# Attention products of the meta tokens and the indexer on 128 contraction rows, and a narrower pooling input

## The chip, the cores and the metric

The kernel runs on one core of a Trainium2 chip. The metric is the device time of one execution in microseconds; a lower time is better. Engines are named as in the profile: PE (TensorE, matmuls), PEld (its weight loads), DVE (VectorE), ACT (ScalarE), POOL (GpSimd), SP (SyncE, which issues the large DMAs).

## What is computed

One layer of a decoder on 256 tokens behind 16 learned meta tokens (272 in all, L), width 2048, in float32. The part that matters here:

```
h = rms_norm(x); q, c_kv, q_idx, k_idx, w_idx, p_in, g_a, g_b = split(h @ w_in)
# indexer: 8 heads of 64; each query keeps the 68 best keys
score[t,s] = sum_h w_idx[t,h] * relu(q_idx[t,h] . k_idx[s] * 64**-0.5), causal
# attention: 16 heads of 128, keys and values from the latent c_kv (256) by w_uk, w_uv
p = softmax(q . (c_kv @ w_uk) * 128**-0.5 over the kept keys);  o = p @ (c_kv @ w_uv)
# pooling: 4 groups of 256 channels, trailing means over 2, 4, 8, 16 tokens minus the token
y[t] = mean(p_in[t-w+1 .. t]) - p_in[t];  b = (y @ w_pool) * scale
merged = sigmoid(g_a) * (o @ w_attn_o) + sigmoid(g_b) * (b @ w_pool_o)
x = x + merged @ w_out;  x = x + relu(rms_norm(x) @ W1)**2 @ W2;  out = rms_norm(x)[16:]
```

## The kernel before

Float32 products are made of three matmuls of a shorter type: each operand is split into a high part (a rounded copy, made by ACT) and a low part (the rest, a subtraction on DVE or POOL), and the product is high x high + high x low + low x high, added up in PSUM. `mm3` (L143 to L146) issues these three; `split_psum`, `split_sbuf` and `split_pair` (L108 to L135) make the two parts of a result.

All weights come in units of 1 MB by SP into three raw buffers. A unit is cut into blocks; `split_block` (L215 to L244) makes a block's two parts, three blocks ahead of its matmuls (four buffers each for high and low). In blocks 20 to 111, POOL makes half of the low part. The last loop of the program walks the list of blocks in order: it converts block i + 3, takes small pieces of side work from a queue (`pop_side`, one piece per block), and issues block i's matmuls. So a piece of side work (normalization, index scores, top-k rounds, attention) stands in PE's queue between two blocks of a large projection, a "slab". Every engine works through its own queue in order.

`slab_t` (L279 to L313) multiplies a slab of 512 columns of weights, transposed, by the 16 chunks of h: per chunk and column tile a 512-wide and a 256-wide matmul (L302, L303), or, where the flag `wide` is set, three matmuls over all 272 tokens (L144 to L146 by `mm3`). Wide are the latent, the index keys and the 8 tiles of the pooling input.

The indexer: its queries (4 tiles, two heads of 64 rows each, `qi`) and its keys (64 rows, held twice in 128 partitions, `kw["k"]`) are split like all else. `score(h)` (L505 to L519) takes the 64 rows of one head, and for each of two query tiles (144 and 272 keys) issues `mm3`; heads are pieces of side work, one per block.

Attention: `kv_block(m)` (L583 to L618), one for each two heads, makes the keys, and the values in three pieces: 16 meta rows, 128 rows, 128 rows. It takes five PSUM banks in turn out of three, so that it waits for evictions. `push_attention` (L620 to L712) queues for each head the scores (s1), the exponentials (s1b), the scaling (s2), the transposition and split of the probabilities (s3, L657 to L676), and the product with the values (s4, L678 to L698): three matmuls on the 16 meta rows, three on the first 128 keys, three on the last 128 keys for the second half of the queries. s3 of one head and s2 of the next are one piece; s4 comes a step after s3.

Pooling: `done_p` (L769 to L776) scales a tile of the pooling input by the token's norm, over all 272 tokens; `pool_tile` (L778 to L802) sums neighbours in doubling steps on POOL.

Of the kernel before, what the change touches and what calls it, by code (L numbers as in the profile page):

```python
# [16 lines left out]
P = 128  # L17
D = 2048
KC = D // P
S = 256  # L20
# [57 lines left out]
def decoder_layer(ctx, tc, x, meta, g_mix, w_in, kv_g, ik_g, w_uk, w_uv, w_ao, w_pool,  # L78
# [11 lines left out]
    early = ExitStack()  # L90
    ptp = early.enter_context(tc.tile_pool(name="ptp", bufs=2))
    fpl = early.enter_context(tc.tile_pool(name="fpl", bufs=1))
    ecst = early.enter_context(tc.tile_pool(name="ecst", bufs=1))
# [185 lines left out]
    def slab_t(w, c0, tiles, rhs, nk=KC, done=None, wide=None, lead=False, more=None):  # L279
# [4 lines left out]
        def mm(k):  # L284
            def go(hi, lo):
                if k == 0:
                    st["ps"] = [gbank() for _ in range(tiles)]
                wides = [wide is not None and wide[j] for j in range(tiles)]
                pss = [st["ps"][j][:, 0:L] if wides[j] else st["ps"][j].rearrange("p (a n) -> p a n", a=2)
                       for j in range(tiles)]  # L290
                todo = [(j, kk) for j in range(tiles) for kk in range(2)]
                if k == 0 and lead:
                    todo.sort(key=lambda jk: jk[1])
                for j, kk in todo:
                    ps = pss[j]
                    xt, o = rhs(k + kk)
                    wh, wl = hi[:, kk, j * P:(j + 1) * P], lo[:, kk, j * P:(j + 1) * P]
                    f, l = k + kk == 0, k + kk == nk - 1
                    if wides[j]:
                        mm3(ps, wh, wl, xt[:, 0, :], xt[:, 1, :], f, l)  # L300
                    else:
                        T.matmul(ps, wh, xt[:, :, o:o + S], start=f, stop=False)  # L302
                        T.matmul(ps[:, 0], wl, xt[:, 0, o:o + S], start=False, stop=l)  # L303
                if k + 2 == nk:
                    jobs = [done(j, pss[j]) for j in range(tiles)]
                    wave(jobs + (more() if more else []))
            return go
# [79 lines left out]
    wn = [cst.tile([P, IH], F32, name=f"wn{t}") for t in range(2)]  # L387

    def done_a1(j, ps):
        if j == 0:  # L390
# [5 lines left out]
        if j == 3:  # L396
            push_kv_norm()
        return split_pair(t, ps)

# [45 lines left out]
    def done_a2(j, ps):  # L445
        if j < 2:
            t = slots.get()
            qi.append(t)
            return split_pair(t, ps)
        kw["raw"] = plain.get()  # L450
# [6 lines left out]
    def push_index():  # L457
# [36 lines left out]
        def s4():  # L494
            kf = env["sq"][:, 1, :]
            kw["k"] = slots.get()
            split_sbuf(kw["k"], kf, L)
            plain.put(env["sq"])
# [6 lines left out]
        def score(h):  # L505
            def go():
                rl = flat(env["rl"][h % 2])
                b = (h % 2) * IDIM
                q, k = qi[h // 2], kw["k"]
                ps = mbank()  # L510
                for t, c0, n in ((0, 0, N0), (1, N0, N1)):
                    qh = q[b:b + IDIM, 0, t * P:(t + 1) * P]
                    ql = q[b:b + IDIM, 1, t * P:(t + 1) * P]
                    mm3(ps[:, c0:c0 + n], qh, ql, k[b:b + IDIM, 0, 0:n], k[b:b + IDIM, 1, 0:n], True, True)
                for t, c0, n in ((0, 0, N0), (1, N0, N1)):
# [5 lines left out]
        def acc(h):  # L521
# [10 lines left out]
                if h == IH - 1:  # L532
# [5 lines left out]
                    for s in qi:  # L538
                        slots.put(s)
                    slots.put(kw["k"])  # L540
                    for s in env["rl"]:
                        plain.put(s)
# [33 lines left out]


    qT = {}
    oT = {}
# [3 lines left out]
    def kv_block(m):  # L583
# [5 lines left out]
        def go(hi, lo):  # L589
# [9 lines left out]
            for o, rows in ((0, NM), (NM, P), (NM + P, P)):  # L599
# [7 lines left out]
                t = slots.get()  # L607
                split_psum(t, ps[0:rows, :], S, rows)
                vv.append(t)
# [10 lines left out]
    def push_attention():  # L620
# [36 lines left out]
        def s3(h):  # L657
            def go():
                sm, _ = env[h]
                f = flat(sm)  # L660
                pt = ptp.tile([P, 2, 640], F32R, tag="pt", name="pt")
                ps = mbank()
# [6 lines left out]
                split_psum(pt, ps[:, 0:384], 384)  # L669
                ptf = pt.bitcast(F32)  # L670
                A.copy(pt[0:NM, 0, 384:640], pz[0:NM, 0:S])
                V.tensor_tensor(out=pt[0:NM, 1, 384:640], in0=pz[0:NM, 0:S], in1=ptf[0:NM, 0, 384:640],
                                op=ALU.subtract)
                plain.put(sm)
                env[h] = pt
            return go  # L676

        def s4(h):  # L678
            def go():
# [4 lines left out]
                o = slots.get()  # L684
                mm3(ps[:, 0:S], vm[0:NM, 0, e:e + DH], vm[0:NM, 1, e:e + DH],
                    pt[0:NM, 0, 384:640], pt[0:NM, 1, 384:640], True, False)
                mm3(ps[:, 0:S], v0[:, 0, e:e + DH], v0[:, 1, e:e + DH], pt[:, 0, 0:S], pt[:, 1, 0:S], False, False)
# [82 lines left out]
    def done_p(s):  # L770
        def go(j, ps):
            i = 4 * s + j
            if i % 2 == 0:
                praw.append(plain.get())
            return [scaled(praw[i // 2][:, i % 2, :], ps, L), lambda: pools.append(i)]
        return go  # L776

    def pool_tile(i):  # L778
# [3 lines left out]
        buf = [tmp[:, 0, :], tmp[:, 1, :]]  # L782
        cur, n, d = p, L, 1
        for lev in range(g + 1):
# [467 lines left out]


    slab_t(w_in, C_KV, 4, rhs_h, done=done_a1, wide=(1, 1, 0, 0), lead=True)
    slab_t(w_in, C_QI + 256, 3, rhs_h, done=done_a2, wide=(0, 0, 1))
    for s in range(3):
# [5 lines left out]
    for s in range(2):  # L1262
        slab_t(w_in, C_P + s * 512, 4, rhs_h, done=done_p(s), wide=(1, 1, 1, 1))
    for s in range(4):
# [158 lines left out]
```

## Time and profile before

| | |
|---|---|
| median of 3 runs | 1411.14 us (1410.97 to 1415.86) |
| the profiled execution | 1411.46 us, its span 1409.7 us |
| PE busy | 1391.6 us (99%), 7664 matmuls |
| PEld busy | 1195.6 us (85%) |
| DVE / ACT / POOL busy | 999.1 / 773.7 / 215.2 us |
| DMA | 264.64 MB, mean 188 GB/s |
| granted TensorE clock | 0.996 of full speed over the span |

The span is the time between the first and the last instruction of the profile. A matmul's busy time runs from its start to its end, and neighbouring matmuls overlap; the pace of a row of matmuls is the distance of their starts.

### The profile page before, as it was taken

What the parts mean: (1) busy time and instruction counts of PE and PEld (TensorE: products, weight loads), DVE (VectorE), ACT (ScalarE), POOL (GpSimd) and SP (SyncE); (2) the same over time, 40 slices, a digit from 0 to 9 for tenths busy, and PEclk for the clock granted to TensorE, in tenths of its full rate; (3) what the DMA queues carried; (4) which work ended last, traced back from release to release, by engine and by line L of the source; (5) the groups of instructions that cost most, each with busy time, mean ns of one, the idle gap of its engine ahead of it and who ended that gap; (6) DMA issues with size and microseconds to landing.
All of it is one profiled execution on the core that took longest, in us unless ns stands there. A gap on an engine that the chain in (4) does not pass through costs nothing.

```text
span 1409.7 us, 19906 instructions
## 1 busy us (share of the span) xinstructions
PE 1391.6 (99%) x7664; PEld 1195.6 (85%) x7664; DVE 999.1 (71%) x1511; ACT 773.7 (55%) x1208; POOL 215.2 (15%) x177
## 2 busy tenths in 40 slices
PE   9999999999999999999999999999999999999997
PEld 7888888899988888888888888888788887788886
DVE  5667965565568766665567887679767788977894
ACT  5655465555555744454465566455555556545562
POOL 1154454444406000000000010000110002000000
PEclk9999999999999999999999999999999999999999
DMA  6654544444446555564555578645787458665562
GB/s 228 198 176 150 165 150 156 145 134 150 150 150 222 200 183 179 198 213 179 179 180 166 196 235 242 204 167 194 220 238 229 157 202 247 236 206 168 195 221 100
DMA packets 125999, 264.64 MB, mean 188 GB/s; under 512 B 5222, under 2 KB 16528, under 8 KB 125904
## 3 DMA queue, kind: packets, MB, share of 16 engines
q1 hardware_dynamic: 120016, 251.68, 52.7%
q0 software_dynamic: 5856, 11.68, 4.1%
q8 instruction: 60, 0.98, 0.3%
q14 instruction: 35, 0.29, 0.1%
q10 hardware_dynamic: 32, 0.01, 0.0%
HBM read 252.86 MB, written 2.10 MB: 181 GB/s over the span
## 4 chain that ended last, share of the span: by engine, by line
PE 75%; issue 12%; DVE 8%; DMA 3%; ACT 1%; POOL 1%; DVEq 0%; ACTq 0%; POOLq 0%
PE g L302 29%; PE g L303 15%; PE g L332 3%; PE g L330 3%; PE g L331 3%; PE m L957 2%; PE m L959 2%; PE m L958 2%; DVE lo L241 2%; PE g L144 2%; PE g L146 2%; PE g L145 2%; PE m L144 1%; DMA raw<-in_w_mlp_out_dram 1%; DVE lo L239 1%
## 5 line engine op out<-in xcount | busy, mean ns | idle before, releaser
L302 PE MATMUL g<-r,hi 128*128 128x512 f32 x2240 | 791.8, 396 | 1.0 <-DVE f L131 1.0
L236 ACT CAST hi<-raw 128x1024 fp32r<-128x1024 f32 (+1 forms) x441 | 455.1, 1045 | 370.1 <-PE g L302 232.1
L303 PE MATMUL g<-r,lo 128*128 128x256 f32 x2240 | 630.5, 281 | 0.6 <-DVE lo L241 0.6
L241 DVE TENSOR_TENSOR lo<-raw,hi 128x1024 fp32r<-128x1024 f32 (+1 forms) x349 | 422.9, 1222 | 245.2 <-ACT hi L236 244.2
L302 PEld LDWEIGHTS g<-r,hi 128*128 128x128 f32 x2240 | 420.9, 188 | 98.2 <-DVE f L131 2.1
L303 PEld LDWEIGHTS g<-r,lo 128*128 128x128 f32 x2240 | 422.9, 189 | 1.1 <-DVE lo L241 0.9
L239 POOL TENSOR_TENSOR lo<-raw,hi 128x512 fp32r<-128x512 f32 x92 | 153.5, 1676 | 213.7 <-ACT hi L236 213.0
L239 DVE TENSOR_TENSOR lo<-raw,hi 128x512 fp32r<-128x512 f32 x92 | 85.4, 929 | 87.5 <-ACT hi L236 87.5
L1067 POOL DMA_DIRECT2D w<-w x32 | 27.8, 1080 | 550.0 <-ACT w L1064 427.5
L957 PE MATMUL m<-hi,r 128*128 128x512 f32 x224 | 89.5, 400 | 0.8 <-ACT w L1064 0.8
L959 PE MATMUL m<-hi,r 128*128 128x512 f32 x224 | 88.6, 396 | 0.0
L958 PE MATMUL m<-lo,r 128*128 128x512 f32 x224 | 88.4, 395 | 0.0
L958 PE MATMUL g<-lo,r 128*128 128x512 f32 x168 | 66.4, 395 | 2.5 <-DVE lo L241 2.3
L130 ACT COPY b<-g 128x256 f32<-128x256 f32 x148 | 54.7, 371 | 25.6 <-PE g L303 20.8
L957 PE MATMUL g<-hi,r 128*128 128x512 f32 x168 | 66.4, 395 | 0.0
L959 PE MATMUL g<-hi,r 128*128 128x512 f32 x168 | 66.4, 395 | 0.0
L330 PE MATMUL g<-hi,r 128*128 128x512 f32 x160 | 64.3, 402 | 0.0
L332 PE MATMUL g<-hi,r 128*128 128x512 f32 x160 | 63.3, 395 | 0.0
L331 PE MATMUL g<-lo,r 128*128 128x512 f32 x160 | 62.5, 390 | 0.0
L144 PE MATMUL g<-r,hi 128*128 128x272 f32 (+1 forms) x192 | 56.9, 296 | 0.0
L236 ACT CAST hi<-ta 128x1024 fp32r<-128x1024 f32 x28 | 29.4, 1051 | 47.8 <-DVE ta L986 29.2
L146 PE MATMUL g<-r,lo 128*128 128x272 f32 (+1 forms) x192 | 55.4, 289 | 0.0
(239 smaller groups left out, 1791.8 us busy)
## 6 DMA issues: line engine op xcount, KB each, us to landing
raw<-in_w_mlp_in_dram SPq DMA_DIRECT2D x64, 1024.0 KB, 5.5
raw<-in_w_mlp_out_dram SPq DMA_DIRECT2D x64, 1024.0 KB, 5.3
raw<-in_w_in_dram SPq DMA_DIRECT2D x56, 1024.0 KB, 5.1
raw<-in_w_attn_o_dram SPq DMA_DIRECT2D x16, 1024.0 KB, 5.1
raw<-in_w_out_dram SPq DMA_DIRECT2D x16, 1024.0 KB, 5.1
raw<-in_w_pool_o_dram SPq DMA_DIRECT2D x8, 1024.0 KB, 5.1
w<-w POOLq DMA_DIRECT2D x32, 256.0 KB, 8.2
raw<-in_w_in_dram SPq DMA_DIRECT2D x8, 512.0 KB, 8.4
```

What stands on the lines that cost most here:

```text
L144: T.matmul(ps, wh, xh, start=first, stop=False)
L236: A.copy(hv, src)
L239: e.tensor_tensor(out=lv[:, kk], in0=src[:, kk], in1=hv.bitcast(F32)[:, kk], op=ALU.subtract)
L241: V.tensor_tensor(out=lv, in0=src, in1=hv.bitcast(F32), op=ALU.subtract)
L302: T.matmul(ps, wh, xt[:, :, o:o + S], start=f, stop=False)
L303: T.matmul(ps[:, 0], wl, xt[:, 0, o:o + S], start=False, stop=l)
L330: T.matmul(ps, xh, hi[:, kk], start=f, stop=False)
L331: T.matmul(ps, xh, lo[:, kk], start=False, stop=False)
L332: T.matmul(ps, xl, hi[:, kk], start=False, stop=l)
L957: T.matmul(ps, xh, wh, start=first, stop=False)
L958: T.matmul(ps, xh, wl, start=False, stop=False)
L959: T.matmul(ps, xl, wh, start=False, stop=last)
```

## The change

The products of the meta tokens and of the index scores are laid out so that the parts of the split lie below each other in the partitions, and one matmul with 128 contraction rows adds up what were several.

- Index queries: `split_heads` puts a head's high and low part into the two halves of the 128 partitions of one plane (even heads plane 0, odd heads plane 1). The high part of the keys lies in both halves already; the low part goes to a second tile `z`, zero but for the half that meets the high queries. Two matmuls per query tile instead of three.
- Meta values: rows 0 to 31, 32 to 63 and 96 to 127 hold the high part (of which 16 rows count), rows 64 to 95 the low part. Meta probabilities go to one of two fixed tiles `pm`, zeroed once: high in rows 0 to 15 and 64 to 79, low in rows 32 to 47. One matmul instead of three.
- Pooling input: `wide` becomes a number of columns. A group with window w computes the last 256 + w tokens (258, 260, 264, 272), two tiles each; `done_p` and `pool_tile` follow.

```diff
@@ slab_t
-                wides = [wide is not None and wide[j] for j in range(tiles)]
-                pss = [st["ps"][j][:, 0:L] if wides[j] else st["ps"][j].rearrange("p (a n) -> p a n", a=2)
+                wides = [wide is not None and wide[j] > 0 for j in range(tiles)]
+                pss = [st["ps"][j][:, 0:wide[j]] if wides[j] else st["ps"][j].rearrange("p (a n) -> p a n", a=2)
...
-                        mm3(ps, wh, wl, xt[:, 0, :], xt[:, 1, :], f, l)
+                        mm3(ps, wh, wl, xt[:, 0, L - wide[j]:], xt[:, 1, L - wide[j]:], f, l)
@@ done_a1, done_a2: split_heads in place of split_pair
+    def split_heads(dst, ps):
+
+        t, st = pair(ps)
+        d = dst.bitcast(F32)
+        lo, hi = slice(0, IDIM), slice(IDIM, P)
+
+        def sub(o, a, b):
+            return lambda: V.tensor_tensor(out=dst[o, b, 0:S], in0=t[a], in1=d[a, b, 0:S], op=ALU.subtract)
+
+        return st + [lambda: A.copy(dst[lo, 0, 0:S], t[lo]), lambda: A.copy(dst[hi, 1, 0:S], t[hi]),
+                     sub(hi, lo, 0), sub(lo, hi, 1)]
@@ push_index, s4
-            split_sbuf(kw["k"], kf, L)
+            z = kw["z"] = slots.get()
+            V.memset(flat(z).bitcast(F32), 0.0)
+            A.copy(kw["k"][:, 0, :], kf)
+            for b, o in ((0, slice(0, IDIM)), (1, slice(IDIM, P))):
+                V.tensor_tensor(out=z[o, b, :], in0=kf[o], in1=kw["k"].bitcast(F32)[o, 0, :], op=ALU.subtract)
@@ score
-                b = (h % 2) * IDIM
-                q, k = qi[h // 2], kw["k"]
+                q, k, z = qi[h // 2], kw["k"], kw["z"]
                 ps = mbank()
                 for t, c0, n in ((0, 0, N0), (1, N0, N1)):
-                    qh = q[b:b + IDIM, 0, t * P:(t + 1) * P]
-                    ql = q[b:b + IDIM, 1, t * P:(t + 1) * P]
-                    mm3(ps[:, c0:c0 + n], qh, ql, k[b:b + IDIM, 0, 0:n], k[b:b + IDIM, 1, 0:n], True, True)
+                    o, qt = ps[:, c0:c0 + n], q[:, h % 2, t * P:(t + 1) * P]
+                    T.matmul(o, qt, k[:, 0, 0:n], start=True, stop=False)
+                    T.matmul(o, qt, z[:, h % 2, 0:n], start=False, stop=True)
@@ before kv_block
+    pms = [mtp.tile([P, S], F32R, name=f"pm{i}") for i in range(2)]
+    for t in pms:
+        V.memset(t.bitcast(F32), 0.0)
@@ kv_block
-                split_psum(t, ps[0:rows, :], S, rows)
+                if rows == NM:
+                    A.copy(t[0:32, 0, 0:S], ps[0:32])
+                    V.tensor_tensor(out=t[64:96, 0, 0:S], in0=ps[0:32], in1=t.bitcast(F32)[0:32, 0, 0:S],
+                                    op=ALU.subtract)
+                    for o in (32, 96):
+                        A.copy(t[o:o + 32, 0, 0:S], ps[0:32])
+                else:
+                    split_psum(t, ps[0:rows, :], S, rows)
@@ s3
-                pt = ptp.tile([P, 2, 640], F32R, tag="pt", name="pt")
+                pt = ptp.tile([P, 2, 384], F32R, tag="pt", name="pt")
...
-                A.copy(pt[0:NM, 0, 384:640], pz[0:NM, 0:S])
-                V.tensor_tensor(out=pt[0:NM, 1, 384:640], in0=pz[0:NM, 0:S], in1=ptf[0:NM, 0, 384:640],
+                pm_ = pms[h % 2]
+                A.copy(pm_[0:NM], pz[0:NM, 0:S])
+                V.tensor_tensor(out=pm_[32:32 + NM], in0=pz[0:NM, 0:S], in1=pm_.bitcast(F32)[0:NM],
                                 op=ALU.subtract)
+                A.copy(pm_[64:64 + NM], pz[0:NM, 0:S])
@@ s4
-                mm3(ps[:, 0:S], vm[0:NM, 0, e:e + DH], vm[0:NM, 1, e:e + DH],
-                    pt[0:NM, 0, 384:640], pt[0:NM, 1, 384:640], True, False)
+                T.matmul(ps[:, 0:S], vm[:, 0, e:e + DH], pms[h % 2], start=True, stop=False)
@@ done_p, pool_tile
-            return [scaled(praw[i // 2][:, i % 2, :], ps, L), lambda: pools.append(i)]
+            n = S + WIN[i // 2]
+            return [scaled(praw[i // 2][:, i % 2, L - n:], ps, n), lambda: pools.append(i)]
...
-        cur, n, d = p, L, 1
+        n, d = S + WIN[g], 1
+        cur = p[:, L - n:]
@@ the slabs
-        slab_t(w_in, C_P + s * 512, 4, rhs_h, done=done_p(s), wide=(1, 1, 1, 1))
+        slab_t(w_in, C_P + s * 512, 4, rhs_h, done=done_p(s), wide=[S + WIN[2 * s + j // 2] for j in range(4)])
```

## Rows read from the trace of the kernel before

**Rows 1.** First part of the page: busy us (share of the span) and instructions by engine.
```profile
PE 1391.6 (99%) x7664; PEld 1195.6 (85%) x7664; DVE 999.1 (71%) x1511; ACT 773.7 (55%) x1208; POOL 215.2 (15%) x177
```

**Rows 2.** Waits of PE: engine, line, releaser, total us, times, longest us.
```profile
PE m L604 <- DVE r L110: 1.7, 3, 1.1
```

**Rows 3.** Busy times by window: length, PE, PEld, DVE, ACT, POOL (instructions), clock, DMA.
```profile
160.00:200.00 40.00, 38.61 (x243) 34.38 (x242) 31.21 (x65) 21.57 (x42) 17.62 (x13) 1.00 0.57 192
```

**Rows 4.** Groups of PE by line and shape: weights, moving operand, count, busy us, mean ns.
```profile
L144 PE MATMUL m<-pt,r 16*128 16x256 f32 x16 | 6.1, 384 | 0.0
...
L144 PE MATMUL m<-r,r 64*128 64x144 f32 x8 | 2.6, 331 | 0.0
```

**Rows 5.** Timeline of PE, 256-column products near the end (start us, duration us); 18 steps.
```profile
1398.06 0.28 PE L352 MATMUL g<-r,r 128*128 128x256 f32 x1
...
1400.17 0.29 PE L352 MATMUL g<-hi,r 128*128 128x256 f32 x1
```

**Rows 6.** Timeline of PE, one head's value products between two slab matmuls.
```profile
232.27 0.28 PE L303 MATMUL g<-r,lo 128*128 128x256 f32 x1
232.47 0.39 PE L144 MATMUL m<-pt,r 16*128 16x256 f32 x1
...
233.49 0.22 PE L144 MATMUL m<-pt,r 128*128 128x128 f32 x1
...
233.77 0.45 PE L302 MATMUL g<-r,hi 128*128 128x512 f32 x1
```

**Rows 7.** Timeline of PE, index scores: the first head, then the last.
```profile
98.34 0.33 PE L145 MATMUL m<-r,r 64*128 64x144 f32 x1 [0.19 <-DVE r L114]
...
128.12 0.28 PE L303 MATMUL g<-r,lo 128*128 128x256 f32 x1
...
129.24 0.50 PE L302 MATMUL g<-r,hi 128*128 128x512 f32 x1
129.57 0.28 PE L303 MATMUL g<-r,lo 128*128 128x256 f32 x1
```

**Rows 8.** Timeline of PE, one head's attention scores up to the second slab matmul.
```profile
210.64 0.23 PE L144 MATMUL m<-r,r 128*128 128x144 f32 x1
...
210.83 0.27 PE L146 MATMUL m<-r,r 128*128 128x144 f32 x1
210.94 0.33 PE L144 MATMUL m<-r,r 128*128 128x272 f32 x1
...
211.35 0.40 PE L302 MATMUL g<-r,hi 128*128 128x512 f32 x1
211.59 0.28 PE L303 MATMUL g<-r,lo 128*128 128x256 f32 x1
```

**Rows 9.** Timeline of DVE: the fill at the start, the low part of the index keys.
```profile
0.84 0.17 DVE L152 MEMSET ones<- 128x128 f32 x1 [0.84 <-PEq L1410]
...
96.76 1.53 DVE L114 TENSOR_TENSOR r<-f,r 128x272 fp32r<-128x272 f32 x1
```

**Rows 10.** Timeline of PE, pooling input, 272 columns; 20 steps.
```profile
329.75 0.29 PE L144 MATMUL g<-r,hi 128*128 128x272 f32 x1
...
332.25 0.29 PE L146 MATMUL g<-r,lo 128*128 128x272 f32 x1
```

**Rows 11.** Groups of ACT by shape: busy us, mean ns, idle us before, releaser.
```profile
L654 ACT ACTIVATE f<-f,st 128x144 f32<-128x144 f32 x16 | 6.7, 416 | 19.2 <-DVE st L653 19.2
...
L671 ACT CAST pt<-m 16x256 fp32r<-16x256 f32 x16 | 5.7, 357 | 0.0
...
L109 ACT CAST r<-m 16x256 fp32r<-16x256 f32 x8 | 2.9, 362 | 1.9 <-PE m L606 1.9
```

**Rows 12.** Timeline of PE at the start, first transpose of the meta tokens.
```profile
6.82 0.23 PE L1344 MATMUL m<-ident,f 16*128 16x16 f32 x1 [0.62 <-DMA f<-in_meta_tokens_dram]
```

**Rows 13.** Timeline of PE and its weight loads at a slab matmul.
```profile
202.02 0.39 PE L302 MATMUL g<-r,hi 128*128 128x512 f32 x1
202.03 0.19 PEld L303 LDWEIGHTS g<-r,lo 128*128 128x128 f32 x1
```

More of the change, by code (lines that the diff above doesn't have):

```diff
@@ L91, in decoder_layer @@
     ptp = early.enter_context(tc.tile_pool(name="ptp", bufs=2))
+    mtp = early.enter_context(tc.tile_pool(name="mtp", bufs=1))
     fpl = early.enter_context(tc.tile_pool(name="fpl", bufs=1))
@@ L397, in done_a1 @@
             push_kv_norm()
-        return split_pair(t, ps)
+        return split_heads(t, ps)
     def push_kv_norm():
@@ L448, in done_a2 @@
             qi.append(t)
-            return split_pair(t, ps)
+            return split_heads(t, ps)
         kw["raw"] = plain.get()
@@ L540, in acc @@
                     slots.put(kw["k"])
+                    slots.put(kw["z"])
                     for s in env["rl"]:
@@ L669, in go @@
                 split_psum(pt, ps[:, 0:384], 384)
-                ptf = pt.bitcast(F32)
-                A.copy(pt[0:NM, 0, 384:640], pz[0:NM, 0:S])
-                V.tensor_tensor(out=pt[0:NM, 1, 384:640], in0=pz[0:NM, 0:S], in1=ptf[0:NM, 0, 384:640],
+                pm_ = pms[h % 2]
+                A.copy(pm_[0:NM], pz[0:NM, 0:S])
+                V.tensor_tensor(out=pm_[32:32 + NM], in0=pz[0:NM, 0:S], in1=pm_.bitcast(F32)[0:NM],
                                 op=ALU.subtract)
+                A.copy(pm_[64:64 + NM], pz[0:NM, 0:S])
                 plain.put(sm)
@@ L1251, in final @@
             nc.sync.dma_start(out=out[t * P:(t + 1) * P, s * 512:(s + 1) * 512], in_=f)
-    slab_t(w_in, C_KV, 4, rhs_h, done=done_a1, wide=(1, 1, 0, 0), lead=True)
-    slab_t(w_in, C_QI + 256, 3, rhs_h, done=done_a2, wide=(0, 0, 1))
+    slab_t(w_in, C_KV, 4, rhs_h, done=done_a1, wide=(L, L, 0, 0), lead=True)
+    slab_t(w_in, C_QI + 256, 3, rhs_h, done=done_a2, wide=(0, 0, L))
     for s in range(3):
```

## The prediction

> **What bounds the kernel now.** I read the busy times first: TensorE is busy for 1391.6 of 1409.7 us, and no other engine comes near it [rows 1]. A busy matmul is not yet a useful one, so the next view is the list of what TensorE waited for: the largest entry that touches the changed code is 1.7 us, in the value products of the key/value blocks, for VectorE [rows 2]. Then the stage in which most of the change lies, from 160 to 200 us: TensorE is busy for 38.61 of 40 us, ScalarE for 21.57, GpSimd for 17.62; only VectorE, with 31.21, is near [rows 3]. So the order of matmuls sets the time, and what an edit is worth is read from start to start of neighbouring matmuls in the timeline, not from their durations: these overlap, so that a removed product is worth far less than its duration, and a pause between two of them isn't in their durations at all. The reader is to see in that view that the matmuls on 16 and 64 rows stand apart from their neighbours by more than a product's pace.
>
> **Meta tokens, 16 heads.** Each head has three products on 16 contraction rows [rows 4] ahead of six on 128. The plain pace of a 256-column product on 128 rows is (1400.17 - 1398.06) / 18 = 0.117 us [rows 5]. From the slab matmul ahead of a head's products to the slab matmul behind them are 233.77 - 232.27 = 1.50 us [rows 6]; the other heads show the same within 0.02. After the change one product on 128 rows takes the place of the three. Then the same stretch is: five steps of 0.117 (slab matmul to meta product, to the three products of the first block of keys, to the first of the second block), and the 0.28 us that the last three products take now, from 233.49 to 233.77 [rows 6]; together 0.865. It saves 0.635 per head, 10.2 us in all. Of this only 2 x 0.117 are columns that are no longer streamed; 0.40 are pauses where the row count changes, at entering and at leaving the 16-row products. That they go is the step that carries the forecast.
>
> **Indexer scores, 8 heads.** Each head has six products on 64 rows [rows 4]; the change makes it four on 128. From the slab matmul ahead of them to the second slab matmul behind them are 129.57 - 128.12 = 1.45 us [rows 7]. For the time after, the trace has a pattern of the same widths on 128 rows, the attention scores: from their first product to the next slab matmul 211.35 - 210.64 = 0.71, then 0.24 to the second slab matmul [rows 8]. Two products go from it, one of 144 columns (0.11 from 210.83 to 210.94) and one of 272 (0.125, below), and 0.117 to enter come on: 0.117 + 0.71 - 0.11 - 0.125 + 0.24 = 0.83. It saves 0.62 per head. Seven heads give 4.3 us. The first head I count at nothing: today its second product waits for VectorE's subtraction (0.19 us idle at 98.34), which takes 1.53 us there, beside GpSimd [rows 7, 9]. After the change a zero fill of 544 columns and a second subtraction stand in the same VectorE queue. The fill is at most 544 / 128 x 0.17 = 0.7 us, an estimate from the fill of 128 columns [rows 9], the subtraction up to another 1.53, so this head may lose up to 1.6 or gain 0.6; nothing is in the middle. Behind it on VectorE stands a weight subtraction for a block some way ahead.
>
> **Pooling input.** Eight tiles take 16 x 3 products each of 272 columns; six of them get narrower, to 258, 260 and 264 columns, two tiles each, so 96 products of each width. At 272 columns the pace is (332.25 - 329.75) / 20 = 0.125 us, at 256 it was 0.117 [rows 5, 10], so 0.49 ns a column: 96 x (14 + 12 + 8) x 0.49 ns = 1.6 us. Below zero is open here: the moving operand then starts 14, 12 or 8 columns into its tile, which no product of this width does today; the last rival has that. The upper bound is these 1.6 us.
> By the Trainium skill (TensorE: Matmul & The Clock Gate, "Back-to-back issue gap") a warm product costs its columns at 2.4 GHz and 2.5 ns, 116 ns at 272 columns, where the trace has 125; the three widths would then be worth 96 x (5.8 + 5.0 + 3.3) ns = 1.4 us, an estimate, and the sum 0.2 us smaller. The trace decides.
>
> **What is added.** On ScalarE: a third copy of the meta probabilities per head, 16 x 0.357, two more copies of the meta values per key/value block, 16 x 0.362 [rows 11], and four more of half the rows where the indexer's queries are split, about 0.36 each: 13 us, spread from 30 to 410 us. The copy per head can be late at most until VectorE's subtraction before it is through; but ScalarE already stands there for VectorE, 19.2 us in 16 waits for the reciprocal that follows that subtraction [rows 11], so only its 0.36 us are new, ahead of weight casts that are made three blocks early. I cost it at nothing. The two copies in a key/value block stand ahead of the evictions of the two larger value banks, and all later weight casts. The next user of the meta bank is a block later. Their bounds are nothing and 8 x 0.72 = 5.8 us; I take 0.5, near the low end, since the three waits on these banks total only 1.7 us [rows 2] and ScalarE idles for 18 of 40 us there [rows 3]. VectorE's added subtractions for the queries (four of half the rows) lie in a stretch without a TensorE wait. The two zero fills of 256 columns at the start, at most 2 x 0.34 us by the same estimate, may push the warm-up matmuls back; they end well before the first meta transpose at 6.82, which waits 0.62 us for its DMA [rows 12]. No DMA is added, removed or moved.
>
> **Sum.** 10.2 + 4.3 + 0 + 1.6 - 0.5 = 15.6 us. The profiled execution took 1411.5 us (span 1409.7), 0.3 above the median of the three runs, so the forecast is 1395.9. What is late next is again TensorE; the chain of weight cast and subtraction has to run 4% faster between 160 and 410 us.
>
> **Rivals.** *The pauses stay* (they belong to freshly written operands, not to the row count): then only columns go, 32 x 0.117 + 7 x 0.235 + 1.6 - 0.5 = 6.5 us, 1405. Against it: the attention scores read fresh tiles too, and enter and leave at the plain pace [rows 8]. Chance 0.05.
> *ScalarE's copies reach TensorE*: the key/value blocks give back all of the 5.8 us, 1401. For it: VectorE, whose subtraction follows each cast, has 9 us of slack in 40 [rows 3], and a cast late by 0.7 us makes it later. Against it: ScalarE's slack. Chance 0.10.
> *The weight loads of the new products come bare*, each 0.19 us longer: 48 remaining new products (32 scores, 16 meta) x 0.19 = 9.1 us, gain 6.5, 1405. Today a load on 128 rows begins at 202.03, inside the product that began at 202.02 and lasts 0.39 [rows 13], so it is hidden. Chance 0.01. Such a rule stands in the Trainium skill (TensorE: Matmul & The Clock Gate, Part 3, "What overlaps and what doesn't"): a load overlaps with a running matmul only where their row groups differ. It speaks for small row groups and against this change; the trace does not agree with it.
> *The pooling products get slower*: if the odd start of the moving operand costs reading time, all 288 pay. Place: the two pooling slabs; the point from which it decides is (15.6 - 1.6) / 288 = 49 ns a product above today's 125. At a halved reading pace, 0.117 us more, it costs 33.7, and 14.0 - 33.7 gives 1431, slower. For it: nothing but that no row has such a start at this width; against it: the slab products already start 16 columns in and keep their pace. Chance 0.03.
> The forecast itself, gains of 12 to 19.5 us, holds 0.80; 0.01 is left for what I don't see.
>
> **Range and chances.** Low end: head 0 gains 0.6, no added cost, and the 1.7 us of waits shrink: 1411.5 - 16.1 - 0.6 - 1.7 = 1393, and 1392 with the reading error of the steps. High end: the second rival, 1401.5. Within 0.5% of the time before (7.1 us, about what a measurement of this kernel can tell from no change) means above 1404: the first and third rival. Faster 0.91 (forecast, second rival, the unseen), same 0.06, slower 0.03.
>
> **What will show it.** In the timeline after: slab matmul to slab matmul 0.87 around a head's value products, 0.83 around a head's index scores up to the second slab matmul, no larger step before the first 128-row product; pooling steps of 0.118 to 0.121. Matmuls fall by 16 + 32, to 7616. TensorE's waits on the value products show whether the 0.5 was right; a ScalarE cast as releaser of weight subtractions more often than now would speak for the second rival. The forecast is wrong if the steps around the changed products stay above 0.2 us, or if the pooling pace rises.

## The result and the profile after

The median of six runs after is 1399.24 us (1398.0 to 1402.9), of six runs before 1411.72 us (1410.97 to 1415.86). The ratio is 0.9909, with a 95% interval from 0.9894 to 0.9923: the medians are 12.5 us apart, and the interval is a gain of 10.9 to 15.0 us. The forecast was 1395.9 us; the kernel is 3.3 us slower than that, and inside the range. The profiled execution of after took 1401.97 us (span 1400.2), so it lies 2.7 us above its median.

The page's first part after, the answer to [rows 1]:

```profile
PE 1380.4 (99%) x7616; PEld 1189.6 (85%) x7616; DVE 1002.4 (72%) x1519; ACT 784.0 (56%) x1244; POOL 214.9 (15%) x177
```

TensorE lost 48 matmuls and 11.2 us of busy time, ScalarE got 36 instructions and 10.3 us. What bounds the kernel is the same. The next view is TensorE's waits after (engine, line, releaser, total us, times, longest us), the answer to [rows 2]; L624 is the old L604:

```profile
PE m L986 <- ACT w L1093: 3.5, 3, 1.3
PE m L624 <- DVE r L111: 2.3, 3, 1.1
PE g L303 <- DVE f L132: 1.3, 3, 0.5
...
PE m L145 <- ACT r L633: 1.0, 4, 0.3
...
PE m L713 <- ACT pm L701: 0.6, 2, 0.4
...
PE m L530 <- DVE r L514: 0.4, 1, 0.4
```

Two entries are new in kind: attention scores (L145) wait for the further copies of the meta values (L633), and value products (L713) for the third copy of the probabilities (L701). Both releasers are ScalarE's added copies. The window of [rows 3] after shows nothing of it:

```profile
160.00:200.00 40.00, 38.32 (x242) 34.28 (x241) 29.97 (x62) 23.38 (x46) 18.38 (x14) 1.00 0.52 172
```

ScalarE is busy for 23.4 of 40 us; it is idle for 16.6 us and late all the same. A share of busy time doesn't tell whether one short instruction comes in time.

Now the timeline of TensorE after, start and duration in us. First one head's value products between two slab matmuls, as in [rows 6]:

```profile
228.48 0.28 PE L304 MATMUL g<-r,lo 128*128 128x256 f32 x1
228.60 0.28 PE L713 MATMUL m<-pm,r 128*128 128x256 f32 x1
...
229.07 0.22 PE L145 MATMUL m<-pt,r 128*128 128x128 f32 x1
...
229.35 0.45 PE L303 MATMUL g<-r,hi 128*128 128x512 f32 x1
```

The stretch is 229.35 - 228.48 = 0.87 us, where it was 1.50. No step ahead of the first product is above 0.12. Then the last head's index scores, as in [rows 7]:

```profile
124.98 0.28 PE L304 MATMUL g<-r,lo 128*128 128x256 f32 x1
125.10 0.23 PE L529 MATMUL m<-r,r 128*128 128x144 f32 x1
...
125.57 0.40 PE L303 MATMUL g<-r,hi 128*128 128x512 f32 x1
125.81 0.28 PE L304 MATMUL g<-r,lo 128*128 128x256 f32 x1
```

To the second slab matmul 0.83 us, where it was 1.45. And ten steps of the pooling products, as in [rows 10]:

```profile
311.84 0.28 PE L146 MATMUL g<-r,hi 128*128 128x258 f32 x1
...
313.04 0.28 PE L147 MATMUL g<-r,lo 128*128 128x258 f32 x1
```

A step of 258 columns is 0.120 us (272 columns: 0.125).

**Where the time went.** The spans of two executions don't resolve 3 us here, so I count another way: the start of a given slab matmul (L302 before, L303 after), measured from the start of the 41st slab matmul of the same execution, which is at 45.0 us before. No slab matmul runs at the last two rows; there it is another product, at 1039 us a 512-wide one (L959 before, L988 after) and at 1402 us the last of the program. How much earlier it comes than before is the lead, in us:

| product at (us, before) | after | after, again | e1 | e2 | e3 | e4 | e5 | e6 | e7 | e8 |
|---|---|---|---|---|---|---|---|---|---|---|
| 132 | 4.86 | 4.88 | 0 | 0 | 4.86 | 0 | 4.88 | 4.88 | 0 | 4.86 |
| 200 | 4.20 | 4.21 | 0 | 0 | 4.76 | -0.69 | 4.63 | 4.64 | 0 | 4.68 |
| 285 | 6.45 | 6.45 | 2.34 | 1.43 | 4.73 | 1.54 | 7.65 | 8.24 | 0 | 8.06 |
| 374 | 9.75 | 9.75 | 4.73 | 2.73 | 4.74 | 3.80 | 11.02 | 13.14 | 1.09 | 12.89 |
| 410 | 11.09 | 11.09 | 6.24 | 3.69 | 4.73 | 5.12 | 13.14 | 15.26 | 1.09 | 14.89 |
| 955 | 10.89 | 10.93 | 6.25 | 3.67 | 4.05 | 5.12 | 12.51 | 14.63 | 0.74 | 14.27 |
| 1039 | 9.35 | 12.97 | 5.68 | 4.40 | 4.75 | 5.21 | 14.21 | 16.02 | 2.19 | 11.00 |
| 1402 | 10.58 | 14.74 | 6.55 | 5.76 | 5.20 | 5.14 | 15.12 | 17.66 | 2.31 | 12.38 |

"After, again" is the same kernel, run and profiled once more: up to 955 us its lead is the first one's within 0.04 us, at 1039 us they are 3.6 us apart. Between the two rows of the table TensorE's granted clock fell to 0.50, the lower of its two levels, for 6.8 us in after and for 3.4 us in before, and not at all in the second run of after; the last section has the rows. So the change is judged by the lead at 410 us, where the last instruction that it touches has been issued: 11.1 us. The profiled span fits: 1409.7 - 10.58, and 1.08 us by which the 41st slab matmul comes later, is 1400.2.

The lead is made up of stretches, each summed from the slab matmul ahead of a side piece to the second one behind it, between 95 and 430 us:

| | before | after | difference |
|---|---|---|---|
| index and attention scores between slab matmuls (17) | 21.37 | 16.53 | -4.84 |
| value products (16) | 28.11 | 19.13 | -8.98 |
| key/value blocks with scores behind them (7) | 35.27 | 38.59 | +3.32 |
| slab matmuls of the pooling input (lead of e7) | | | -1.09 |
| rest, waits of slab matmuls near 255 us among it | | | +0.5 |

Without the last two heads, which wait for ScalarE, the value products would be 10.14 less (16 x 0.635); the two add 1.16. So 4.84 + 10.14 + 1.09 = 16.1 us were gained and 5.0 given back, in place of 0.5.

The give-back in the timeline of all engines after, at a key/value block and the head's scores behind it (out<-in; the bracket is the idle time ahead and what ended it):

```profile
277.29 0.36 ACT L629 CAST r<-m 32x256 fp32r<-32x256 f32 x1 [0.32 <-PE m L626]
...
277.69 0.42 DVE L630 TENSOR_TENSOR r<-m,r 32x256 fp32r<-32x256 f32 x1 [0.24 <-ACT r L629]
...
278.14 0.73 ACT L633 CAST r<-m 32x256 fp32r<-32x256 f32 x2 [0.48 <-DVE r L630]
...
278.40 0.28 PE L626 MATMUL m<-hi,r 128*128 128x256 f32 x1
278.92 0.34 PE L145 MATMUL m<-r,r 128*128 128x144 f32 x1 [0.24 <-ACT r L633]
```

ScalarE makes the first copy of the meta values, VectorE subtracts, and only then does ScalarE make the two further copies, although these need nothing of the subtraction. They end at 278.87; the attention scores want the meta bank at 278.52, one step behind the block's last product, and start at 278.92, 0.40 us late, with a second step of 0.18 us where a plain one is 0.07. In all it costs 0.50 to 0.59 us in six of the seven blocks, 0.14 in the first. In the second and third the longer wait for VectorE (L624, 2.3 us in all where it was 1.7) has a share in it. At the last two heads the same with the probabilities:

```profile
388.00 0.41 DVE L699 TENSOR_TENSOR pm<-m,pm 16x256 fp32r<-16x256 f32 x1
...
388.45 0.36 ACT L701 CAST pm<-m 16x256 fp32r<-16x256 f32 x1 [1.57 <-DVE pm L699]
...
388.86 0.39 PE L713 MATMUL m<-pm,r 128*128 128x256 f32 x1 [0.23 <-ACT pm L701]
```

The groups of ScalarE by shape (busy us, mean ns, idle us ahead and its releaser) show how general that is, also where TensorE is not reached:

```profile
L633 ACT CAST r<-m 32x256 fp32r<-32x256 f32 x16 | 5.8, 362 | 5.5 <-DVE r L630 5.4
...
L701 ACT CAST pm<-m 16x256 fp32r<-16x256 f32 x16 | 5.8, 361 | 21.4 <-DVE pm L699 21.4
```

### The profile page after: what moved, and what is told of

It reads as the page before. It is cut to its first block, busy times and chain, and to the rows that moved or that the text cites. A ratio compares the mean times of both kernels' runs of the same rounds, so it can differ in the third digit from the quotient of the medians.

```text
span 1400.2 us, 19865 instructions
## 1 busy us (share of the span) xinstructions
PE 1380.4 (99%) x7616; PEld 1189.6 (85%) x7616; DVE 1002.4 (72%) x1519; ACT 784.0 (56%) x1244; POOL 214.9 (15%) x177
## 4 chain that ended last, share of the span: by engine, by line
PE 77%; issue 10%; DVE 8%; DMA 2%; ACT 2%; POOL 0%; DVEq 0%; ACTq 0%; POOLq 0%
PE g L303 30%; PE g L304 15%; PE g L333 3%; PE g L331 3%; PE g L332 3%; PE m L986 3%; PE m L988 3%; PE m L987 3%; DVE lo L242 2%; PE g L145 2%; PE g L146 2%; PE g L147 2%; PE g L987 2%; PE g L988 2%; PE g L986 2%
## 5 line engine op out<-in xcount | busy, mean ns | idle before, releaser
L303 PE MATMUL g<-r,hi 128*128 128x512 f32 x2240 | 791.1, 396 | 1.3 <-DVE f L132 1.3
L303 PEld LDWEIGHTS g<-r,hi 128*128 128x128 f32 x2240 | 420.9, 188 | 97.7 <-DVE f L132 2.5
L986 PE MATMUL m<-hi,r 128*128 128x512 f32 x224 | 89.4, 399 | 2.2 <-ACT w L1093 2.2
L988 PE MATMUL m<-hi,r 128*128 128x512 f32 x224 | 88.7, 396 | 0.0
L988 PE MATMUL g<-hi,r 128*128 128x512 f32 x168 | 66.5, 396 | 0.0
L986 PE MATMUL g<-hi,r 128*128 128x512 f32 x168 | 66.5, 396 | 0.0
L145 PE MATMUL g<-r,hi 128*128 128x272 f32 (+4 forms) x192 | 56.8, 296 | 0.0
L146 PE MATMUL g<-r,hi 128*128 128x272 f32 (+4 forms) x192 | 55.3, 288 | 0.0
```

Of the source, the lines that this page charges most:

```text
L145: T.matmul(ps, wh, xh, start=first, stop=False)
L986: T.matmul(ps, xh, wh, start=first, stop=False)
L988: T.matmul(ps, xl, wh, start=False, stop=last)
```

## The experiments

The diffs are against before in e1, e2 and e7 and against after in the others, and show the lines that matter; the rest is left out.

Two theories stood to begin with for the pauses (they belong to the row count, or to freshly written operands), and two for the give-back: the *order* (copies queue behind a subtraction that they don't need, and the bank is freed late) and *early arrival* (TensorE reaches these places earlier by the scores' gain, and meets evictions that would have been late anyway).

**e1, three meta products as before, but on 128 rows.** The meta values are split over all 128 rows and the probabilities lie in tiles that are zero below row 16; scores and pooling are those of before.

```diff
-                split_psum(t, ps[0:rows, :], S, rows)
+                split_psum(t, ps, S)
@@ s4
-                mm3(ps[:, 0:S], vm[0:NM, 0, e:e + DH], vm[0:NM, 1, e:e + DH],
-                    pt[0:NM, 0, 384:640], pt[0:NM, 1, 384:640], True, False)
+                mm3(ps[:, 0:S], vm[:, 0, e:e + DH], vm[:, 1, e:e + DH], pm_[:, 0], pm_[:, 1], True, False)
```

> The kernel before, with the meta tokens' three products per head kept, but on 128 contraction rows: the value tile takes all 128 rows of its PSUM bank, the probabilities go to two tiles zeroed once. No copy, subtraction or matmul is added. Theory (the pauses belong to the change of the row count): the stretch from slab matmul to slab matmul around a head's value products falls from 1.50 to 7 x 0.117 + 0.28 = 1.10 us, 16 x 0.40 = 6.4 us less, about 1405.3. Rival (they belong to freshly written operands, or to three products more): the stretch stays at 1.50 and the time at 1411.7.

1405.83 us (ratio 0.9953, 0.9938 to 0.9968), lead 6.24. TensorE around one head's value products:

```profile
233.19 0.28 PE L304 MATMUL g<-r,lo 128*128 128x256 f32 x1
233.31 0.28 PE L145 MATMUL m<-pm,r 128*128 128x256 f32 x1
...
234.30 0.44 PE L303 MATMUL g<-r,hi 128*128 128x512 f32 x1
```

The same nine products take 1.11 us instead of 1.50: 0.39 us went with the row count alone, and the operands are as fresh as before. The key/value blocks are at 35.29 us: a split into the same number of instructions gives nothing back.

**e2, one meta product, left on 16 rows.** The other half of the same question.

```diff
-                mm3(ps[:, 0:S], vm[0:NM, 0, e:e + DH], vm[0:NM, 1, e:e + DH],
-                    pt[0:NM, 0, 384:640], pt[0:NM, 1, 384:640], True, False)
+                T.matmul(ps[:, 0:S], vm[0:NM, 0, e:e + DH], pt[0:NM, 0, 384:640], start=True, stop=False)
```

> The kernel before, with one meta product per head on 16 rows in place of three: high x low and low x high of the meta tokens are left out. Theory (row count): both pauses stay, the stretch falls only by two columns' worth, 1.50 - 0.235 = 1.27 us, 3.8 us less in all, about 1408. Rival (each small product brings its own pause): the stretch falls to about 0.9, 10 us less, about 1402.

1407.77 us (0.9966, 0.9955 to 0.9977), lead 3.69. TensorE and its weight loads (PEld) at one head:

```profile
232.31 0.28 PE L303 MATMUL g<-r,lo 128*128 128x256 f32 x1
232.52 0.18 PEld L685 LDWEIGHTS m<-pt,r 16*128 16x128 f32 x1 [0.25 <-issue]
232.52 0.38 PE L685 MATMUL m<-pt,r 16*128 16x256 f32 x1
...
232.83 0.19 PEld L144 LDWEIGHTS m<-pt,r 128*128 128x128 f32 x1
232.83 0.38 PE L144 MATMUL m<-pt,r 128*128 128x256 f32 x1
232.94 0.19 PEld L145 LDWEIGHTS m<-pt,r 128*128 128x128 f32 x1
233.05 0.28 PE L145 MATMUL m<-pt,r 128*128 128x256 f32 x1
...
233.57 0.45 PE L302 MATMUL g<-r,hi 128*128 128x512 f32 x1
```

1.26 us where one product on 128 rows takes 0.87. A single product on 16 rows keeps both pauses: the step into it is 0.21, the step out of it 0.31, and the one behind the first product on 128 rows 0.22, where a plain step is 0.117; together they exceed it by 0.39. So of the 0.635 us per head 0.24 are columns and 0.39 pauses, as forecast. The weight loads show where a pause lies: the load of the first product behind a change of the row count starts with that product (232.52, 232.83), the next one 0.11 us ahead of its own (232.94 for 233.05). In before it is so at all 48 changes of the row count between 95 and 430 us, in and out of 16 heads' value products and 8 heads' index scores: the load starts 1 or 2 ns ahead of its product, where nine in ten of the other loads start 110 ns ahead or more. So a load of 0.18 or 0.19 us, about the size of the pause, isn't hidden there; whether the load makes the product late or something else holds back both, no run separates. The Trainium skill (TensorEngine Tiling (Array Packing), "Key Properties") says that a change of the tiling mode drains TensorE. If 16 rows count as another mode, which the trace can't say, these rows agree, and they give the price: some 0.2 us each way.

**e3, the index scores alone.** Meta tokens and pooling as before.

```diff
+                split_psum(t, ps[0:rows, :], S, rows)
@@ s4
+                mm3(ps[:, 0:S], vm[0:NM, 0, e:e + DH], vm[0:NM, 1, e:e + DH],
+                    pt[0:NM, 0, 384:640], pt[0:NM, 1, 384:640], True, False)
```

> Of the change, the index scores alone. Both theories: 1.45 to 0.83 us a head, some 4.8 us less, about 1407. They differ behind 130 us. Theory (the new waits in attention come from ScalarE's copies, which stand behind VectorE's subtraction): no new wait, the lead of 4.8 us stays to the end. Rival (TensorE now comes early into a stretch where VectorE is nearly full and waits there): the value products of the key/value blocks wait longer than the 1.7 us of before, and about 1 us is given back by 230 us.

1407.06 us (0.9969, 0.9953 to 0.9985), lead 4.73 at 410 us. The same wait as in [rows 2] is unchanged:

```profile
PE m L620 <- DVE r L110: 1.7, 3, 1.1
```

TensorE reaches the key/value blocks 4.86 us earlier here, and they take 35.35 us, 0.08 more than before. Early arrival falls: alone it gives back 0.13 us at most (the lead goes from 4.86 at 132 us to 4.73 at 410 us).

**e4, the meta tokens alone.** Index scores and pooling as before.

```diff
-            return split_heads(t, ps)
+            return split_pair(t, ps)
@@ push_index, score
+            split_sbuf(kw["k"], kf, L)
...
+                    mm3(ps[:, c0:c0 + n], qh, ql, k[b:b + IDIM, 0, 0:n], k[b:b + IDIM, 1, 0:n], True, True)
```

> Of the change, the meta tokens alone, copies included. Theory (ScalarE's copies): 10.2 us are won in the stretches and about 3.5 given back, in the attention scores right behind a key/value block (4 x 0.4), in the last heads (1.0) and in the value products of the blocks (0.6): 6.5 less, about 1405. Rival (early arrival in a full VectorE): without the scores' lead the give-back is under 1.5, 9 us less, about 1402.5.

1406.9 us (0.9963, 0.9950 to 0.9976), lead 5.12; 10.14 less 5.12 is a give-back of 5.0 us, larger than I had expected. Its waits:

```profile
PE m L620 <- DVE r L111: 2.3, 3, 1.1
...
PE m L145 <- ACT r L629: 1.0, 4, 0.3
...
PE m L709 <- ACT pm L697: 0.7, 2, 0.4
```

They are those of after (L620 is L624 there, L629 L633, L709 L713), with no gain of the scores ahead of them, and the key/value blocks take 38.60 us. So the give-back belongs to the meta tokens' own evictions. The kernel is behind before at 200 us (-0.69) and ahead only when more heads' products have come.

**e5, all copies ahead of the subtraction.** If the order is the cause, ScalarE should be through before VectorE.

```diff
-                    A.copy(t[0:32, 0, 0:S], ps[0:32])
+                    for o in (0, 32, 96):
+                        A.copy(t[o:o + 32, 0, 0:S], ps[0:32])
                     V.tensor_tensor(out=t[64:96, 0, 0:S], in0=ps[0:32], in1=t.bitcast(F32)[0:32, 0, 0:S],
                                     op=ALU.subtract)
-                    for o in (32, 96):
-                        A.copy(t[o:o + 32, 0, 0:S], ps[0:32])
@@ s3
+                A.copy(pm_[64:64 + NM], pz[0:NM, 0:S])
                 V.tensor_tensor(out=pm_[32:32 + NM], in0=pz[0:NM, 0:S], in1=pm_.bitcast(F32)[0:NM],
                                 op=ALU.subtract)
-                A.copy(pm_[64:64 + NM], pz[0:NM, 0:S])
```

> The changed kernel with ScalarE's extra copies issued ahead of VectorE's subtraction, in the key/value blocks and in the split of the probabilities; nothing else differs. Theory (the give-back is the wait of the later copies for that subtraction, and what stands behind them): the last two heads no longer wait for the probabilities (1.2 us back); in the key/value blocks the bank is free when the subtraction is through, which now follows three copies, about 0.15 us earlier than before in each of seven (1 us back): 2 us less than the changed kernel. Rival (the copies' own time on ScalarE is the cost, in any order): no difference.

1397.87 us (0.9894, 0.9879 to 0.9909), lead 13.14, which is 2.05 more than after, as expected. The last two heads give 0.76 of their 1.16 back, the key/value blocks 0.86, of which 0.75 in the first three; the remaining 0.4 is the rest of the table above. In the later blocks the wait only changes its owner:

```profile
276.56 1.11 ACT L630 CAST r<-m 32x256 fp32r<-32x256 f32 x3 [0.32 <-PE m L626]
...
277.70 0.41 DVE L631 TENSOR_TENSOR r<-m,r 32x256 fp32r<-32x256 f32 x1 [0.99 <-ACT r L630]
...
278.17 0.33 PE L145 MATMUL m<-r,r 128*128 128x144 f32 x1 [0.22 <-DVE r L631]
```

Now the subtraction stands behind all three copies, although it needs the first alone, and it releases the bank. The order was only half the cause: as long as the copies and the subtraction read the same bank, they don't run beside each other in either order.

**e6, one copy in place of three.** The meta columns of the latent are laid out four times, once, ahead of the blocks; the product then writes the meta values into all four groups of 32 rows, one copy of 128 rows makes the high parts, and the subtraction takes rows 64 to 95. The copies of the probabilities are in e5's order.

```diff
+                m4 = mtp.tile([P, 2, P], F32R, name=f"m4_{cc}")
+                for pl in range(2):
+                    A.copy(m4[:, pl].rearrange("p (q n) -> p q n", q=4),
+                           t.bitcast(F32)[:, pl, 0:32].unsqueeze(1).to_broadcast([P, 4, 32]))
+                ckm.append(m4)
@@ kv_block
-                    A.copy(t[0:32, 0, 0:S], ps[0:32])
-                    V.tensor_tensor(out=t[64:96, 0, 0:S], in0=ps[0:32], in1=t.bitcast(F32)[0:32, 0, 0:S],
+                    A.copy(t[:, 0, 0:S], ps)
+                    V.tensor_tensor(out=t[64:96, 0, 0:S], in0=ps[64:96], in1=t.bitcast(F32)[64:96, 0, 0:S],
                                     op=ALU.subtract)
-                    for o in (32, 96):
-                        A.copy(t[o:o + 32, 0, 0:S], ps[0:32])
```

> The changed kernel with no extra copy in the key/value blocks: the latent's 16 meta columns (and 16 more) stand four times side by side in a small tile that is made once, so that the matmul itself puts the meta values into all four quarters of the PSUM bank; then one copy of 128 rows and one subtraction of 32, as many as in the kernel before. The probabilities' copies go ahead of the subtraction. Theory: the seven key/value pieces with scores behind them fall from 38.6 to the 35.3 us of before, the last two heads stop waiting, 0.4 of the slab waits goes: 4.6 us less than the changed kernel, about 1394.6. Rival (the give-back is TensorE's earlier arrival): no more than 1 us.

1395.05 us (0.9878, 0.9863 to 0.9894), lead 15.26, 4.17 more than after. Of these, 2.9 are in the key/value blocks (35.70 us) and 0.8 at the last two heads, as in e5; the remaining 0.5 is the rest of the table. It is the fastest kernel of this study, 4.1 us below the same chip's run of after (1399.17). The scores follow the block at the plain pace, without a wait:

```profile
277.37 0.28 PE L632 MATMUL m<-hi,r 128*128 128x256 f32 x1
...
277.49 0.23 PE L145 MATMUL m<-r,r 128*128 128x144 f32 x1
```

**e7, the pooling input alone.**

```diff
+        slab_t(w_in, C_P + s * 512, 4, rhs_h, done=done_p(s), wide=[S + WIN[2 * s + j // 2] for j in range(4)])
```

> Of the change, the pooling input alone. By the pace forecast, 1.6 us less in the two pooling slabs; by the pace in the changed kernel (120, 120, 122 ns against 125) 96 x (5 + 5 + 3) ns = 1.25 us. Rival (something else in the change pays for the pooling): the lead behind the pooling slabs differs from 1.25 by more than 0.3 us. The whole time may not tell it from no change.

1410.85 us against 1411.8 (0.9991, 0.9981 to 1.0001); its time can't be told from no change, but its lead can: 1.09 us at 374 us, 0.74 at 955. It differs from the 1.25 expected by 0.16, so that rival falls. The three parts add up: 4.73 + 5.12 + 1.09 = 10.94 of 11.09.

**e8, the further copies read the first copy, not the bank.** The order of after is kept, word for word but for the source.

```diff
-                        A.copy(t[o:o + 32, 0, 0:S], ps[0:32])
+                        A.copy(t[o:o + 32, 0, 0:S], t.bitcast(F32)[0:32, 0, 0:S])
...
-                A.copy(pm_[64:64 + NM], pz[0:NM, 0:S])
+                A.copy(pm_[64:64 + NM], pm_.bitcast(F32)[0:NM])
```

> The changed kernel in its own order (copy, subtraction, further copies), but the further copies read the first copy in SBUF, not the PSUM bank. It asks what makes them wait for the subtraction. If it is the shared PSUM bank: the copies no longer wait, the bank is free after the subtraction, and at 410 us the kernel leads the changed one by 2 to 4 us. If it is the shared output tile: they wait as in the changed kernel, the bank alone is free earlier (0.4 x 4 in the attention scores behind key/value blocks), the last two heads still wait, and the lead is 1.5 to 2 us.

1396.71 us (0.9888, 0.9871 to 0.9904), lead 14.89, 3.80 more than after. The same block in the timeline:

```profile
275.09 0.36 ACT L629 CAST r<-m 32x256 fp32r<-32x256 f32 x1 [0.32 <-PE m L626]
...
275.48 0.82 ACT L633 CAST r<-r 32x256 fp32r<-32x256 f32 x2
275.48 0.42 DVE L630 TENSOR_TENSOR r<-m,r 32x256 fp32r<-32x256 f32 x1 [0.24 <-ACT r L629]
...
276.32 0.23 PE L145 MATMUL m<-r,r 128*128 128x144 f32 x1
```

Copies and subtraction start in the same moment, and the scores don't wait. The idle time ahead of the copies falls from 5.5 to 0.3 us and from 21.4 to 0.5 us, although the copies themselves got longer (0.40 us in place of 0.36). So what held them was the shared bank, not the shared output tile: where a copy by ScalarE and the subtraction by VectorE read the same rows of one bank, one stands behind the other. The Trainium skill (PSUM — Partial Sum Buffer, "Terms") says that two engines must not use one bank and group of 32 partitions at once, reads against reads included. The rows of after and e5 agree, in that no two such reads overlap, and in e8 the further copies read no bank. It is the program that keeps them apart: in the trace's instructions of after the first of the further copies waits for semaphore 101, which the subtraction L630 raises; in e8 it waits for 118, which ScalarE's own first copy raises. What the chip does without such a wait, no run shows.

## Why the prediction was right, and where its terms were off

*The pauses go* (10.2 forecast). 0.635 us a head, 10.14 in all, where nothing waits. The mechanism is shown by e1 and e2, and with it the first rival fell: fresh operands on 128 rows have no pause.

*The scores* (4.3 forecast). 4.84. Seven heads take 0.83 us, as forecast. The first head, costed at nothing, went from 1.86 to 1.43; its queue on VectorE after:

```profile
97.98 0.51 DVE L511 MEMSET r<- 128x544 f32 x1
...
98.60 1.23 DVE L514 TENSOR_TENSOR r<-f,r 64x272 fp32r<-64x272 f32 x2
...
99.41 0.34 PE L530 MATMUL m<-r,r 128*128 128x144 f32 x1 [0.38 <-DVE r L514]
```

Only the first of the two half subtractions stands ahead of this head's product (98.60 to 99.36; the second serves the odd heads). It takes 0.76 us, where the one of before took 1.53 [rows 9], but the zero fill of 0.51 us (up to 0.7 forecast) stands ahead of it, and TensorE's wait is 0.38 us where it was 0.19. The pauses that went were worth more. The head lies inside the bounds that were given.

*The pooling* (1.6 forecast). 1.09. The paces are 0.120 us at 258 and at 260 columns, 0.122 at 264, where 0.118, 0.119 and 0.121 were forecast; 96 x (5 + 5 + 3) ns is 1.25. By the formula of the Trainium skill (TensorE: Matmul & The Clock Gate, "Back-to-back issue gap"), which the page gives for a single matmul by itself, it would have been 1.4, an estimate; the traces lie below both. The rival of slower pooling products fell: the odd start costs 2 ns a product at the most.

*The added work* (0.5 forecast, bounds 0 to 5.8). 5.0: 3.32 in the key/value blocks, 1.16 at the last two heads, and the rest of 0.5, in which slab matmuls that wait for VectorE (L303, 1.3 us where it was 1.0) have a part. This is the term that was mis-sized, and two sentences of it failed.
"The next user of the meta bank is a block later" was wrong: a head's scores follow most blocks in TensorE's queue at once and take that bank, which the rows of the timeline behind a block would have shown.
The copy of the probabilities, costed at nothing "because ScalarE already stands there for VectorE", was right for 14 heads. At the last two the value products follow so soon that VectorE's subtraction came just in time before; now a copy of 0.36 us stands between that subtraction and the product.
The time is inside the range because the range reached up to the second rival: the gains came as forecast (16.1, with 0.5 more from the scores and 0.5 less from the pooling, which cancel by luck), and the added work ended near its upper bound, not at the 0.5 that was taken.

*The second rival* (ScalarE's copies reach TensorE, all of 5.8 us) happened for the most part in size, 3.3 and 1.2 us, but by another path. It had the copies delay weight casts by their own duration. What happened is that copies of 0.36 us were held back by a subtraction that reads the same bank, and that this bank was wanted next; e8 keeps every copy and has 3.8 of the 5.0 us back. That the size came near the bound of 5.8 is in part luck: the bound was the copies' own duration, which isn't what was paid. *Bare weight loads* fell for the new products, which follow at 0.12 us; in before the loads lay bare at the changes of the row count (e2), so there they were, if anything, a reason for the change.

Not settled: the key/value blocks of e6 and e8 still take 0.43 and 0.47 us more than before, in the second and third of them, where the wait for VectorE of [rows 2] is 2.2 and 2.1 us in place of 1.7; the last two heads' value products still take 0.4 us (e5, e6) and 0.5 us (e8) more than two others; the kernels e5 to e8 lose some 0.37 us of lead between 440 and 600 us, which after does not. I tried nothing for any of these. Of the two further copies in a key/value block one fills rows 96 to 127, where the probabilities are zero, so it adds nothing to the product; no run leaves it out.

## What to carry to other kernels

Read pauses from start to start where the row count of neighbouring matmuls changes: a few rows that are padded with zeros to 128, or filled with the parts of a split, can cost less than a small product. Before further reads of a PSUM bank are queued, look in the timeline for who wants that bank next and which engine's read stands in between; read copies of a copy from SBUF, or have the matmul write all the rows that one copy takes. Where runs scatter more than the effect, compare the start of one and the same matmul ahead of the change and behind it, and read the granted clock of both executions.

## What the runs showed of the hardware

The executions differ in when TensorE is at the lower of its two clock levels (1.2 and 2.4 GHz), and a part of what the spans scatter by lies there.

At the start, matmuls of 272 columns follow at 0.23 us instead of 0.125, up to 11.8 us before and 13.5 us after. In before the record of the granted clock is at half from 8.3 to 11.7 us, with TensorE busy throughout (window: length, busy us by engine, granted clock, DMA share, GB/s):

```profile
8.40:11.70 3.30, 3.30 (x12) 2.71 (x12) 2.71 (x6) 2.74 (x5) 0.00 (x0) 0.50 1.06 346
```

For after the same view prints full clock:

```profile
9.00:15.00 6.00, 6.00 (x27) 5.16 (x27) 3.42 (x6) 2.45 (x6) 0.00 (x0) 1.00 1.05 381
```

But its matmuls run at the lower pace in this window, one at 12.65 us, the next at 12.88:

```profile
12.65 0.43 PE L146 MATMUL g<-r,hi 128*128 128x272 f32 x1
```

The record of after begins only at 13.55 us, and the view counts time without a record as full clock. So a 1.00 in this column is to be checked against the steps; where there is a record, it agrees with the steps of 272 and 512 columns in all traces, single steps aside. It turns to full at 11.7 us before, 12.0 in e8 and 15.2 in e7, and the 41st slab matmul comes at 45.0, 45.0 and 46.9 us.

A second such stretch lies near 1000 us. Granted clock in after, then in its second run:

```profile
1000.02:1006.82 6.80, 5.93 (x13) 4.25 (x14) 5.10 (x6) 3.72 (x5) 0.86 (x1) 0.50 0.84 183
```

```profile
1000.00:1007.00 7.00, 6.24 (x27) 4.84 (x28) 6.91 (x8) 4.03 (x5) 0.00 (x0) 1.00 1.03 257
```

In after TensorE was idle for 3.5 us in three waits for ScalarE just ahead of it (L986 in the list above), and 512-wide products follow at 0.43 us in this stretch, at 0.23 to 0.24 us behind it. At half the clock 6.8 us cost 3.4 us, an estimate from the two steps, which is most of the 3.6 us between the two runs at 1039 us. In before the stretch is 3.4 us long, from 1011.8 to 1015.2 us.
